# A two-block transformer on one core: the low-part splits of the second block's weights all on VectorE

## The chip, the cores and the metric

The kernel runs on one core of one Trainium2 chip. The time is device microseconds of one execution; a kernel's time is the median of several. One further execution was taken with the profiler, and every row below is from it. Engines are called PE (TensorE matmul), PEld (its weight loads), DVE (VectorE), ACT (ScalarE), POOL (GpSimd) and SP (SyncE), as in the profile.

## The reference

Everything is float32, with 512 tokens of width 1024. A first block (a gated delta-rule branch and a windowed-attention branch over 512 tokens and a context of 256, merged) hands its result `h` to a second block, which has two layers. A layer is

```
h = h + 0.5*rmsnorm(swiglu(rmsnorm(h,g0)), g1)      # feed-forward, 1024 -> 2816 -> 1024
h = h + rmsnorm(mixer(rmsnorm(h,g2)), g3)           # latent attention and dilated attention
h = h + 0.5*rmsnorm(swiglu(rmsnorm(h,g4)), g5)      # a second feed-forward
h = h + rmsnorm((p @ w_ple) * sigmoid(rmsnorm(h,g6) @ w_gate), g7)
```

## The kernel before

Activations lie transposed, features on partitions and tokens along the row. A float32 product is made of three matmuls in float32r: each operand is written as a high part H and a low part L = value - H, and H·H, H·L and L·H are summed in PSUM (`fm`, `acc` at line 87).

**Weights.** Every weight tile of 128x1024 goes the same way, in `w` (lines 70 to 85): a DMA from SP's queue brings it into `wraw`; ACT copies it to `wH` (line 78); then `wL = wraw - wH` is made at line 80, on VectorE where the letter `l` is "v", the default, and on GpSimd where it is "g". In the second block there are 8 pairs of `wH` and `wL` to go round and 3 `wraw`.

**Stages of a layer.** `ffn` runs over the 22 blocks of 128 of the hidden width in three parts (8, 7 and 7), and after each part multiplies by the down weights and adds into `f`. The last down product is made by halves of 256 tokens, so that the norms of the first half run while PE still works on the second. `norms` and `prenorm` are, for a half: a sum of squares over 8 tiles (ACT squares at lines 156 and 159, DVE adds them at line 160, PE sums at line 133), an inverse square root in some 14 tiny DVE instructions (`rsq`, lines 112 to 124), a broadcast by PE (line 141), then for each of 8 tiles DVE's `nt` (line 191) and `h` (line 193) with a new sum of squares; a second inverse square root; and for each of 8 tiles `ny` (line 171), ACT's `xnH` (line 101) and DVE's `xnL` (line 105). Only then has PE an input for the next stage. The next stage begins by halves too: `ffn` takes its first four hidden blocks (8 weight tiles) for the first half and then for the second, `ple` its 8 gate tiles, `mixer` the latent projections and the values of the dilated branch.

**Who splits where.** The letter "g" stands, in the second block, at just these beginnings: 8 tiles at the start of each of the four `ffn` (the calls of `gw` in part 0), 4 tiles `wvd` in each of the two `mixer`, 8 tiles `wpg` in each of the two `ple`: 56 tiles. All other weights of the second block are split on DVE. The first block has 36 tiles on GpSimd.

**Order.** The program is written in the order of the stages, and the compiler's planner (a list scheduler with estimated costs) then decides the order of instructions on each engine, with the program's order as priority. A queue runs strictly in the planned order: an instruction that waits holds back all behind it on its engine. In the trace such splits are seen among the instructions of the norms that precede them in the program.

Of the kernel before, what the change touches and what calls it, by code (L numbers as in the profile page):

```python
# [26 lines left out]
class Kern:  # L27
# [1027 lines left out]
    def ffn(self, l, j, g_out, g_next):  # L1055

        nc, I = self.nc, self.I
        X = (self.xnH, self.xnL)
        with ExitStack() as ctx:
            p = self.pool(ctx, "ffn", 1)  # L1060
            f = self.f
            NA = 4
            A = {}

            def gu(W, ff, c):
                if ff not in A:
                    A[ff] = tuple(p.tile([128, T], F32R, name="a" + z, bufs=9) for z in "HL")
                pg, pu = self.ps("g"), self.ps("x")
                n = c[1] - c[0]
                self.acc(pg[:, :n], self.fm(W[0], X, range(8), 0, c))  # L1070
                self.acc(pu[:, :n], self.fm(W[1], X, range(8), 0, c))
                s = p.tile([128, T], F32, name="fs", bufs=2)[:, :n]
                a = p.tile([128, T], F32, name="fa", bufs=2)[:, :n]
                nc.scalar.activation(s, pg[:, :n], AF.Silu)
                nc.vector.tensor_tensor(a, s, pu[:, :n], op=ALU.mult)  # L1075
                self.split(A[ff][0][:, c[0]:c[1]], A[ff][1][:, c[0]:c[1]], a, h="v")

            def gw(ff, l2="vv"):
                return [self.w(I["gu"][l, j, ff, z], 8, 128, l=l2[z]) for z in range(2)]

            ss = [self.SumSq(self) for _ in HALVES]

            def down(W, part, dm, c):
                k0, k1 = PARTS[part]
                n = c[1] - c[0]
                ps = self.ps("x" if dm % 2 else "g")
                prs = []
                for k in range(k0, k1):
                    aH, aL = A[k]
                    prs += [(W[0][:, k - k0], aH[:, c[0]:c[1]]), (W[0][:, k - k0], aL[:, c[0]:c[1]]),  # L1090
                            (W[1][:, k - k0], aH[:, c[0]:c[1]])]
                self.acc(ps[:, :n], prs)
                fk = f[:, dm, c[0]:c[1]]
                if part == 0:
                    nc.scalar.activation(fk, ps[:, :n], AF.Copy)
                else:
                    nc.vector.tensor_tensor(fk, fk, ps[:, :n], op=ALU.add)
                if part == len(PARTS) - 1:
                    ss[0 if c[0] == 0 else 1].add(fk)

            def dw(part, dm):
                k0, k1 = PARTS[part]
                return self.w(I["dn%d" % part][l, j, dm], k1 - k0, 128)

            for part, (k0, k1) in enumerate(PARTS):
                ffs = list(range(k0, k1))
                if part == 0:
                    ws = {ff: gw(ff, "gg") for ff in ffs[:NA]}
                    for c in HALVES:
                        for ff in ffs[:NA]:  # L1110
                            gu(ws[ff], ff, c)
                            self.pull(4)
                        self.pull()
                    ffs = ffs[NA:]
                for ff in ffs:
                    gu(gw(ff), ff, (0, T))
                if part < len(PARTS) - 1:
                    for dm in range(8):
                        down(dw(part, dm), part, dm, (0, T))
                else:  # L1120
                    ws = [dw(part, dm) for dm in range(8)]
                    for z, c in enumerate(HALVES):
                        for dm in range(8):
                            down(ws[dm], part, dm, c)
                            self.pull(2)
                        self.later(self.norms(ss[z], c, f, g_out, 0.5, g_next))
# [81 lines left out]
    def mixer(self, l, G):  # L1208

        nc, I = self.nc, self.I  # L1210
# [5 lines left out]
        with ExitStack() as ctx:  # L1216
# [5 lines left out]
            gg = p.tile([128, 8], F32, name="gg")  # L1222
# [75 lines left out]
            with ExitStack() as c2:  # L1298
# [5 lines left out]
                latH = p2.tile([128, 3, T], F32R, name="latH")  # L1304
                latL = p2.tile([128, 3, T], F32R, name="latL")
                ws = [self.w(I["win"][l, z], 8, 128) for z in range(3)] + [self.w(I["wkr"][l], 8, 64)]
                wv = [[self.w(I["wvd"][l, g, z], 4, 256, l="g") for z in range(2)] for g in range(2)]
                kr = [p2.tile([32, T], F32, name="kr%d" % z) for z in range(2)]
                for c in HALVES:
                    n = c[1] - c[0]  # L1310
# [138 lines left out]
            ws = []  # L1449
# [20 lines left out]
    def ple(self, l, G, g_next):  # L1470

        nc, I = self.nc, self.I
        X = (self.xnH, self.xnL)
        with ExitStack() as ctx:
            p = self.pool(ctx, "ple", 1)
            f = self.f
            last = g_next is None
            ws, pe = [], []
            for c in HALVES:
                ss = self.SumSq(self)  # L1480
                for dm in range(8):
                    if c[0] == 0:
                        ws.append(self.w(I["wpg"][l, dm], 8, 128, l="g"))
                        pe.append(p.tile([128, T], F32, name="pe", bufs=8))
                        nc.sync.dma_start(pe[dm], self.ple_dram[l, dm])
                    ps = self.ps("x" if dm % 2 else "g")[:, :256]
                    self.acc(ps, self.fm(ws[dm], X, range(8), 0, c))
                    t = p.tile([128, 256], F32, name="pt", bufs=2)
                    nc.scalar.activation(t, ps, AF.Tanh, scale=0.5)
                    fk = f[:, dm, c[0]:c[1]]  # L1490
                    nc.vector.scalar_tensor_tensor(fk, t, 1.0, pe[dm][:, c[0]:c[1]], op0=ALU.add, op1=ALU.mult)
                    ss.add(fk, 0.5)
                    self.pull(2)
                self.later(self.norms(ss, c, f, G[7], 0.5, g_next, out=self.O["out"] if last else None))
# [254 lines left out]
```

## Time and profile before

| | |
|---|---|
| median of 3 runs | 3103.57 us (3096.75 to 3115.26) |
| the profiled execution, its own time | 3092.88 us |
| its span from the first to the last instruction | 3090.7 us |
| granted TensorE clock, mean over the span | 0.948 of full speed |
| PE, DVE, ACT, POOL busy | 90%, 56%, 35%, 15% |

The profiled execution lies 10.7 us under the median of the three runs. Its time is 2.2 us more than its span. A granted clock of 1.0 is 2.4 GHz, and the only other level in this trace is 0.5 (1.2 GHz).

### The profile page before, as it was taken

The page shows a single profiled execution, that of the slowest core. Times are in us where ns is not written, and L with a number is a line of the kernel's source. Part 1 is how long each engine was busy: PE and PEld are TensorE (multiplying, and loading weights), DVE is VectorE, ACT ScalarE, POOL GpSimd, SP SyncE. Part 2 cuts the span into 40 slices and gives each one's busy share as a digit, 9 for nine tenths or more (in the row PEclk, how much of TensorE's full clock was granted, in tenths as well). Part 3 has the DMA queues.
Part 4 walks back from the last instruction along what each step waited for, and adds up shares of the span by engine and source line. Part 5 has one row for each costly group of instructions (what it writes and reads, how often), then busy time and mean ns, then how long its engine had stood idle before and what let it go on. Part 6 is the DMA issues. An engine that isn't in the chain of part 4 may idle for free.

```text
span 3090.7 us, 41787 instructions
## 1 busy us (share of the span) xinstructions
PE 2795.3 (90%) x15792; PEld 2357.2 (76%) x15792; DVE 1727.9 (56%) x3701; ACT 1082.1 (35%) x2078; POOL 460.2 (15%) x361
## 2 busy tenths in 40 slices
PE   6999698998999986978999988999987887999987
PEld 2877577678888984768888888888886667888887
DVE  6678927666333474668423378433375567623357
ACT  3444235533222232664322233222232474322223
POOL 3024212322000022412000022000011332000010
PEclk8999899999999997999999998999998898999998
DMA  5325341433323147743323221333234763233321
GB/s 192 102 98 170 103 147 49 136 134 116 96 89 100 54 145 204 187 155 100 116 92 99 89 83 56 118 94 97 86 108 136 217 200 114 88 96 92 97 78 55
DMA packets 138017, 354.51 MB, mean 115 GB/s; under 512 B 36912, under 2 KB 41392, under 8 KB 136792
## 3 DMA queue, kind: packets, MB, share of 16 engines
q1 hardware_dynamic: 125752, 316.18, 33.9%
q10 hardware_dynamic: 9216, 23.07, 2.3%
q0 software_dynamic: 2848, 12.59, 1.2%
q8 instruction: 124, 2.03, 0.3%
q14 instruction: 77, 0.63, 0.1%
HBM read 296.21 MB, written 55.57 MB: 114 GB/s over the span
## 4 chain that ended last, share of the span: by engine, by line
PE 69%; DVE 15%; issue 6%; DMA 4%; ACT 4%; POOL 2%; SPq 0%; DVEq 0%; ACTq 0%; POOLq 0%
PE psg L87 30%; PE psx L87 27%; PE psn L87 3%; DVE ss L160 2%; PE psx L1196 1%; DVE big L529 1%; DVE wL L80 1%; PE psn L141 1%; DMA wraw<-in_wo 1%; DVE h L193 1%; ACT wH L78 1%; DVE rq_y L120 1%; DVE xnL L105 1%; DVE cy L403 1%; PE psn L133 1%
## 5 line engine op out<-in xcount | busy, mean ns | idle before, releaser
L78 ACT ACTIVATE wH<-wraw 128x1024 fp32r<-128x1024 f32 (+2 forms) x445 | 445.0, 1003 | 1149.5 <-PE psg L87 571.7
L80 DVE TENSOR_TENSOR wL<-wraw,wH 128x1024 fp32r<-128x1024 f32 (+3 forms) x353 | 407.9, 1157 | 452.0 <-ACT wH L78 451.2
L87 PE MATMUL psg<-xnH,wH 128*128 128x512 f32 (+3 forms) x1528 | 544.5, 358 | 13.5 <-ACT ss L156 6.8
L87 PE MATMUL psg<-xnL,wH 128*128 128x512 f32 (+3 forms) x1528 | 544.5, 357 | 9.1 <-DVE xnL L105 9.1
L87 PE MATMUL psg<-xnH,wL 128*128 128x512 f32 (+3 forms) x1528 | 546.4, 358 | 6.3 <-POOL wL L80 5.5
L80 POOL TENSOR_TENSOR wL<-wraw,wH 128x1024 fp32r<-128x1024 f32 x92 | 226.6, 2468 | 1896.6 <-ACT wH L78 1068.8
L87 PE MATMUL psx<-xnH,wL 128*128 128x512 f32 (+1 forms) x1120 | 389.0, 348 | 2.8 <-POOL wL L80 1.7
L87 PE MATMUL psx<-xnH,wH 128*128 128x512 f32 (+1 forms) x1120 | 389.9, 348 | 1.7 <-ACT wH L78 1.6
L87 PE MATMUL psx<-xnL,wH 128*128 128x512 f32 (+1 forms) x1120 | 389.7, 348 | 0.0
L87 PEld LDWEIGHTS psg<-xnH,wH 128*128 128x128 f32 (+2 forms) x1528 | 294.5, 193 | 53.6 <-ACT ss L156 7.2
L87 PEld LDWEIGHTS psg<-xnL,wH 128*128 128x128 f32 (+2 forms) x1528 | 295.3, 193 | 49.8 <-DVE xnL L105 12.0
L87 PEld LDWEIGHTS psg<-xnH,wL 128*128 128x128 f32 (+2 forms) x1528 | 295.4, 193 | 46.9 <-POOL wL L80 6.6
L87 PEld LDWEIGHTS psx<-xnH,wL 128*128 128x128 f32 x1120 | 214.9, 192 | 29.9 <-POOL wL L80 1.9
L87 PEld LDWEIGHTS psx<-xnH,wH 128*128 128x128 f32 x1120 | 215.2, 192 | 28.9 <-ACT wH L78 2.3
L87 PEld LDWEIGHTS psx<-xnL,wH 128*128 128x128 f32 x1120 | 215.1, 192 | 25.8
L1075 DVE TENSOR_TENSOR fa<-fs,psx 128x512 f32<-128x512 f32 (+1 forms) x104 | 62.9, 605 | 269.6 <-PE psx L87 268.7
L87 PE MATMUL psg<-aH,wH 128*128 128x512 f32 (+1 forms) x464 | 160.0, 345 | 0.0
L87 PE MATMUL psg<-aL,wH 128*128 128x512 f32 (+1 forms) x464 | 159.3, 343 | 0.0
L87 PE MATMUL psg<-aH,wL 128*128 128x512 f32 (+1 forms) x464 | 159.0, 343 | 0.0
L87 PE MATMUL psx<-aL,wH 128*128 128x512 f32 (+1 forms) x464 | 158.7, 342 | 0.0
L87 PE MATMUL psx<-aH,wL 128*128 128x512 f32 (+1 forms) x464 | 158.2, 341 | 0.0
L87 PE MATMUL psx<-aH,wH 128*128 128x512 f32 (+1 forms) x464 | 158.2, 341 | 0.0
(568 smaller groups left out, 4792.6 us busy)
## 6 DMA issues: line engine op xcount, KB each, us to landing
wraw<-in_gu SPq DMA_DIRECT2D x176, 512.0 KB
wraw<-in_dn SPq DMA_DIRECT2D x64, 448.0 KB
wraw<-in_dn SPq DMA_DIRECT2D x32, 512.0 KB
wraw<-in_wmod SPq DMA_DIRECT2D x24, 512.0 KB
wraw<-in_wrest ACTq DMA_DIRECT2D x24, 512.0 KB
wraw<-in_wo SPq DMA_DIRECT2D x24, 512.0 KB
wraw<-in_win SPq DMA_DIRECT2D x22, 512.0 KB
kh<-KD SPq DMA_DIRECT2D x32, 256.0 KB
```

Source lines behind the costliest of these rows:

```text
L78: nc.scalar.activation(H[:, :n], raw[:, :n], AF.Copy)
L80: e.tensor_tensor(L[:, :n], raw[:, :n], H[:, :n].bitcast(F32), op=ALU.subtract)
L87: self.nc.tensor.matmul(ps, lhsT=l, rhs=r, start=start and i == 0, stop=stop and i == m - 1)
L105: e.tensor_tensor(L, src, H.bitcast(F32), op=ALU.subtract)
L120: nc.vector.scalar_tensor_tensor(z, b, 1.5, y, op0=ALU.add, op1=ALU.mult)
L133: self.nc.tensor.matmul(ps[:, 2 * c:2 * c + 2], lhsT=a[:, 128 * c:128 * c + 128], rhs=self.ones2[:a.shape[0]], start=i == 0, stop=i == len ...
L141: self.nc.tensor.matmul(ps[:, 128 * c:128 * c + 128], lhsT=rs[:, c:c + 1].to_broadcast([128, 128]), rhs=self.ident, start=True, stop=True)
L160: nc.vector.tensor_tensor(self.a[i], self.a[i], q, op=ALU.add)
L193: nc.vector.tensor_tensor(hk, hk, t, op=ALU.add)
L403: nc.vector.scalar_tensor_tensor(y, cb[:, o + j:o + j + n], cw[:, j:j + 1], y, op0=ALU.mult, op1=ALU.add)
L529: nc.vector.tensor_tensor(tm, A[:112, i:i + 1, i + 1:].to_broadcast([112, n, n]), A[:112, i + 1:, i + 1:].rearrange("q j c -> q c j"), op= ...
L1075: nc.vector.tensor_tensor(a, s, pu[:, :n], op=ALU.mult)
```

## The change

The letter "g" is dropped in the second block at all three places, so that the 56 low parts that GpSimd made are made by VectorE. Nothing else is edited: the tiles, their buffers, the DMAs and ACT's copies stay. The first block keeps its 36 splits on GpSimd, and GpSimd keeps its other work (rotary sums, the scaling of attention weights, some DMA issues).

```diff
-            def gw(ff, l2="vv"):
-                return [self.w(I["gu"][l, j, ff, z], 8, 128, l=l2[z]) for z in range(2)]
+            def gw(ff):
+                return [self.w(I["gu"][l, j, ff, z], 8, 128) for z in range(2)]
...
-                    ws = {ff: gw(ff, "gg") for ff in ffs[:NA]}
+                    ws = {ff: gw(ff) for ff in ffs[:NA]}
...
-                wv = [[self.w(I["wvd"][l, g, z], 4, 256, l="g") for z in range(2)] for g in range(2)]
+                wv = [[self.w(I["wvd"][l, g, z], 4, 256) for z in range(2)] for g in range(2)]
...
-                        ws.append(self.w(I["wpg"][l, dm], 8, 128, l="g"))
+                        ws.append(self.w(I["wpg"][l, dm], 8, 128))
```

## Rows read from the trace of the kernel before

**Rows 1.** The page: busy time by engine; the chain that ended last, by engine.
```profile
PE 2795.3 (90%) x15792; PEld 2357.2 (76%) x15792; DVE 1727.9 (56%) x3701; ACT 1082.1 (35%) x2078; POOL 460.2 (15%) x361
...
PE 69%; DVE 15%; issue 6%; DMA 4%; ACT 4%; POOL 2%; SPq 0%; DVEq 0%; ACTq 0%; POOLq 0%
```

**Rows 2.** Groups by shape, second block: busy us, mean ns, idle before, its releasers.
```profile
L80 DVE TENSOR_TENSOR wL<-wraw,wH 128x1024 fp32r<-128x1024 f32 x222 | 272.1, 1226 | 321.5 <-ACT wH L78 320.9
...
L80 POOL TENSOR_TENSOR wL<-wraw,wH 128x1024 fp32r<-128x1024 f32 x56 | 136.4, 2442 | 1741.1 <-ACT wH L78 923.8 <-DVE rq_a L118 704.7 <-DVE ny L171 44.2
```

**Rows 3.** Eight stretches with these splits: length, PE, PEld, DVE, ACT, POOL busy, clock.
```profile
700.00:736.00 36.00, 27.36 (x208) 26.18 (x208) 30.91 (x55) 16.33 (x30) 19.52 (x8) 0.95 0.33 103
...
1792.00:1834.00 42.00, 27.80 (x210) 26.90 (x209) 37.05 (x74) 16.28 (x30) 19.11 (x8) 0.88 0.37 112
...
sum 384.00, PE 295.90 PEld 284.79 DVE 325.86 ACT 165.49 POOL 137.55; mean PE 36.99 PEld 35.60 DVE 40.73 ACT 20.69 POOL 17.19
```

**Rows 4.** POOL in order of time, first feed-forward end of layer 0: start, length.
```profile
1796.45 2.35 POOL L80 TENSOR_TENSOR wL<-wraw,wH 128x1024 fp32r<-128x1024 f32 x1 [352.25 <-DVE rq_a L118]
```

**Rows 5.** DVE in order of time, the same stretch.
```profile
1796.18 0.16 DVE L118 TENSOR_TENSOR rq_a<-rq_v,rq_y 128x2 f32<-128x2 f32 x1
1796.37 0.16 DVE L119 SCALAR_TENSOR_TENSOR rq_b<-rq_a,rq_y 128x2 f32<-128x2 f32 x1
1796.57 2.25 DVE L120 SCALAR_TENSOR_TENSOR rq_y<-rq_b,rq_y 128x2 f32<-128x2 f32 x1
...
1821.19 2.43 DVE L160 TENSOR_TENSOR ss<-ss,ss_q 128x256 f32<-128x256 f32 x1 [0.29 <-ACT ss_q L159]
```

**Rows 6.** DVE groups of the second block, by shape: busy, mean ns.
```profile
L160 DVE TENSOR_TENSOR ss<-ss,ss_q 128x256 f32<-128x256 f32 x248 | 132.3, 540 | 34.5 <-ACT ss_q L159 33.0
L105 DVE TENSOR_TENSOR xnL<-ny,xnH 128x256 fp32r<-128x256 f32 x160 | 82.0, 551 | 9.1 <-ACT xnH L101 8.6
...
L193 DVE TENSOR_TENSOR h<-h,nt 128x256 f32<-128x256 f32 x112 | 61.8, 578 | 0.0
```

**Rows 7.** The same lines from 700 us on: ns shortest/median/longest.
```profile
L160 DVE TENSOR_TENSOR ss<-ss,ss_q x240: 402/419/2654, 702.6 to 3074.5; 128x256 f32<-128x256 f32 x120
...
L105 DVE TENSOR_TENSOR xnL<-ny,xnH x160: 407/417/2657, 699.9 to 3053.3; 128x256 fp32r<-128x256 f32 x160
...
L193 DVE TENSOR_TENSOR h<-h,nt x112: 405/417/2622, 1070.0 to 3040.0; 128x256 f32<-128x256 f32 x112
```

**Rows 8.** The chain that ended last, 1792 to 1834 us: start, us, what.
```profile
1811.66 2.10 DVE ss L160
1813.76 2.48 DVE h L193
...
1833.47 0.62 PE psg L87 x3
```

**Rows 9.** PE's waits, first feed-forward (690 to 800), then 1780 to 1850: us, times, longest.
```profile
PE psg L87 <- POOL wL L80: 4.5, 3, 1.9
PE psx L87 <- POOL wL L80: 1.7, 1, 1.7
...
PE psn L133 <- DVE ss L160: 7.9, 2, 7.7
```

**Rows 10.** DVE's waits for a split's high part: 1385 to 1450, and 2575 to 2645.
```profile
DVE wL L80 <- ACT wH L78: 5.1, 3, 1.8
...
DVE wL L80 <- ACT wH L78: 4.2, 3, 1.9
```

**Rows 11.** DVE splits at the first mixer's start, then one inside an inverse square root.
```profile
1066.85 1.23 DVE L80 TENSOR_TENSOR wL<-wraw,wH 128x1024 fp32r<-128x1024 f32 x1
...
1392.62 1.23 DVE L80 TENSOR_TENSOR wL<-wraw,wH 128x1024 fp32r<-128x1024 f32 x1 [1.51 <-ACT wH L78]
```

**Rows 12.** ACT's waits with the splits' copies, 1785 to 1835.
```profile
ACT wH L78 <- PE psx L87: 5.8, 2, 4.4
ACT wH L78 <- PE psg L87: 4.7, 2, 2.4
```

## The prediction, made before the changed kernel was built or run

> **What bounds the kernel now.** I read the page first. PE is busy for nine tenths of the span and the chain that ended last lies on it for 69%, on DVE for 15% and on POOL for 2% [rows 1]. So only what PE waits for can be won or lost, and it has to be looked for where the 56 splits stand. Order of time on POOL put them into eight stretches, all at the turn of one stage to the next: six with 8 splits (each feed-forward's start, each gate stage's start), two with 4 (the mixers). Together the stretches are 384 us long, PE works 295.9 us of them and DVE 325.9 [rows 3]. Here PE is idle for 88.1 us, and here DVE, not PE, is the fullest engine: 37.05 of 42 us in the fourth stretch. There PE runs out of the old stage's products while the norms, which make the input of the next stage, go step by step through DVE; its longest waits name a DVE sum [rows 9]. The chain confirms it: from 1796 us to the first matmul of the next stage at 1833 us it runs almost without a break over DVE [rows 8].
>
> Then I laid POOL and DVE of one stretch side by side, and this decides the case. POOL starts a split at 1796.45 and takes 2.35 us [rows 4]. DVE's tiny steps took 0.16 us until then; the one that starts at 1796.57 takes 2.25 us, to within 0.1 us of the end of POOL's split [rows 5]. A sum that usually takes 0.42 us takes 2.43 us beside another split. All eight splits of this stretch have such a stretched DVE instruction, and the long pieces of the chain [rows 8] are these. So a split on POOL is not taken off DVE. DVE stands still for most of it, and loses more than the 1.23 us that the same split takes on DVE itself [rows 2].
>
> **The change part by part.**
>
> *The stall that goes.* Lower bound: the three commonest lines of the norms have medians of 419, 417 and 417 ns [rows 7] and means of 540, 551 and 578 [rows 6]; the excess is 248 x 0.121 + 160 x 0.134 + 112 x 0.161 = 30.0 + 21.4 + 18.0 = 69.4 us, 1.24 us a split. Inverse square root steps, stretched too [rows 5], are not in it. Upper bound: the two stretched instructions of rows 5, 2.25 - 0.16 and 2.43 - 0.42, or 2.0 us a split, 112 us. I take 1.7 us, nearer to the upper, since the tiny steps are missing below: 56 x 1.7 = 95.2 us that DVE gets back.
>
> *The splits that come.* 56 x 1.226 us [rows 2] = 68.7 us on DVE. POOL loses 136.4 us of work, which nobody waits for except in the first stretch. On DVE alone that is 95.2 - 68.7 = 26.5 us less. Nothing hides it: the stalls lie on the chain [rows 8], and the splits will lie among the same instructions. The planner puts a split wherever DVE is free by its estimate, as it did with the mixer's own splits in the midst of the norms [rows 11].
>
> *The part of the splits in DVE's idle time.* DVE is idle for 58.1 us of the 384, or 15% [rows 3], in pieces in which it waits for PE or ACT. Bounds: none of the splits' time falls there, or 58.1 us of it. A split of 1.23 us mostly overlaps such a piece in part; I take the share by chance, 15% of 68.7, or 10.3 us gained.
>
> *The wait that comes.* On POOL a split that waited for ACT's copy held up nobody. On DVE it holds all the norm steps queued behind it, so ACT's next squares, PE's sum and the next stage. Bounds for one split: nothing, as at the first mixer's start [rows 11], and 1.55 us, as the six waits of 9.3 us in all of the output weights' splits at two other turns [rows 10]. One of these stood inside an inverse square root and cost 1.51 us there [rows 11]. What ACT itself waits for in the fourth stretch is a buffer that PE must free, 10.5 us in four waits [rows 12]. But ACT's queue is held by these waits already, and its squares with it, so a good part is in the present time. I take 0.25 us a split, near the lower bound since most splits there had no wait: 14 us lost.
>
> *The first stretch.* Here PE waited for POOL's splits outright, 4.5 + 1.7 = 6.2 us [rows 9]. A split of 1.23 in place of 2.44 us halves that: 3 us gained; bounds 0 and 6.2.
>
> *TensorE's clock.* In the fourth stretch the granted clock is 0.88 on average [rows 3]: with levels of 1.0 and 0.5 that is 10 us of 42 at 1.2 GHz, beside gaps of PE. Shorter gaps should give some of it back. Bounds: none, and half of those 10 us in each of eight stretches, 40 us, which would need no gaps at all. I take 3 us.
>
> *What costs nothing.* The DMAs, their queues and ACT's copies are unchanged in number and order of need. POOL's DMA issues lose what stood ahead of them. The 36 splits of the first block, and POOL's other work, stay as they are.
>
> Sum: -26.5 - 10.3 + 14 - 3 - 3 = -28.8 us. The profiled execution took 3092.9 us (its span and 2.2 us around it), so 3064.1 by its own time. It lay 10.7 us under the median of the runs shown; by that median the forecast is 3075 us.
>
> A rule of the Trainium skill speaks against the change: Perfetto Trace Analysis, Optimizing Scalar/DVE Operations, says that work of a saturated DVE may sensibly be offloaded, even to GpSimd. It adds that the two share a read port, so that moving work between them might not help. By the first half alone the 68.7 us would simply be added to DVE, a result that stands below as the fourth rival. The stretched instructions of rows 5 bear out the second half.
>
> **The rivals.**
>
> *Splits wait at the head of DVE's queue, slower.* Place: the six stretches with 8 splits, where ACT's copy waits for a buffer that PE frees. For it speaks that the planner works with estimates and that these waits exist [rows 10, 12]. Against it: today's POOL stalls, which hit DVE at the moment the copy is done, disturb the planned order more. It decides from 0.25 + 28.8 / 56 = 0.76 us of wait a split on; at the 1.55 us of rows 10 for all 56 the loss is 56 x 1.30 - 28.8 = 44 us, or 3148 us.
>
> *The stalls are hidden, no change.* The stretched instructions might lie beside PE's work, with another wait ending last. For it: PE is at work in 77% of the stretches [rows 3]. Against it: the chain [rows 8]. The time would be 3104 us, 15 more or less.
>
> *The splits vanish in DVE's pauses, a larger gain.* If 58.1 us of them fall into idle time, nothing waits and the two small terms hold, the sum is -95.2 + 10.6 - 6 = -90.6 us. That is more than PE's idle 88.1 us, part of which is the norms' own length; I put it at two thirds of it, 60 us, or 3044 us.
>
> *DVE's stall is not POOL's doing, slower.* Then the change gives nothing back and adds 68.7 - 10.3 + 14 - 6 = 66 us: 3170 us. Against it stands the match in time of rows 4 and 5, eight times in a stretch.
>
> **How the numbers follow.** The forecast, a gain of 10 to 50 us, has 0.57; its centre is the predicted time. The larger gain has 0.10, no change 0.15, waits at the head of the queue 0.15, the fourth 0.03. About 0.5%, or 15.5 us, is what a measurement of this kernel can tell from no change. Faster: 0.10, 0.50 of the forecast and 0.02 of no change's lower edge, 0.62. Within: 0.07 of the forecast, 0.12 of no change and 0.01 of a weak wait, 0.20. Slower: 0.14 + 0.03 and the upper edge of no change, 0.18. The range goes from 3040, the larger gain's middle, to 3112, past no change: outside are half of the larger gain, most of the two slower cases and a little of the others, 2 in 10. The likeliest case alone would be 3055 to 3093.
>
> **What would show it.** Right: no DVE instruction of the norms longer than about 0.5 us in the eight stretches, means of lines 160, 105 and 193 near 0.42 us, 278 splits of 1024 columns on DVE from 680 us on at about 1.23 us; the chain from the sum at 1793 us to the next stage's first matmul shorter than its 40 us by some 3 to 7 us; PE's idle time in the stretches down from 88 to about 60 us; the other stages as they were. Wrong: DVE's waits for the high part in these stretches adding up to more than 40 us (the first rival), PE's gaps as long as before with DVE emptier (the second), or DVE instructions still stretched with no GpSimd work beside them (the fourth). The prediction also fails if the planner, given other costs, sets the norms of the two halves in another order, so that PE gets its first input later.

## The result, and the profile after

The changed kernel takes 3058.61 us (median of 4 runs, 3055.07 to 3066.91) beside 3101.34 us for the kernel before: a ratio of 0.9862, with a 95% interval of 0.9828 to 0.9896, or 42.7 us less. It is faster, as forecast; the range of 3040 to 3112 us holds it, and the forecast of 3075 us was 16 us too slow. The range is 72 us wide and holds the kernel before as well, so that it was hit says little; the sign had a chance of 0.62.

The page of the changed kernel, with the busy time by engine and the chain that ended last by engine:

```profile
span 3054.4 us, 41703 instructions
PE 2800.5 (92%) x15792; PEld 2361.5 (77%) x15792; DVE 1682.6 (55%) x3757; ACT 1083.3 (35%) x2078; POOL 324.0 (11%) x305
...
PE 74%; DVE 12%; issue 4%; DMA 4%; ACT 4%; POOL 2%; SPq 0%; DVEq 0%; ACTq 0%; POOLq 0%
```

DVE ran 56 instructions more and is busy 45.3 us less than in [rows 1]; its share of the chain fell from 15% to 12%. Groups of the second block by shape, with the mean in ns behind the time that they took in sum, show where from:

```profile
L80 DVE TENSOR_TENSOR wL<-wraw,wH 128x1024 fp32r<-128x1024 f32 x279 | 341.3, 1225 | 339.3 <-ACT wH L78 338.9
L160 DVE TENSOR_TENSOR ss<-ss,ss_q 128x256 f32<-128x256 f32 x250 | 103.9, 424 | 31.7 <-ACT ss_q L159 30.4
...
L105 DVE TENSOR_TENSOR xnL<-ny,xnH 128x256 fp32r<-128x256 f32 x160 | 60.5, 420 | 9.1 <-ACT xnH L101 8.8
...
L193 DVE TENSOR_TENSOR h<-h,nt 128x256 f32<-128x256 f32 x112 | 43.4, 419 | 0.0
```

The means of 540, 551 and 578 ns [rows 6] became 424, 420 and 419, within 5 ns of the medians of [rows 7]. The longest `h`, 2622 ns before, is now 425 (ns shortest/median/longest of the line):

```profile
L193 DVE TENSOR_TENSOR h<-h,nt x112: 416/419/425, 1069.9 to 3002.1; 128x256 f32<-128x256 f32 x112
```

In the fourth stretch the first layer's second feed-forward ends and its gate stage begins ([rows 4] call it the first feed-forward, but the weights loaded in it are the gate's). There the chain of the changed kernel (start, us, what) reads:

```profile
1786.80 0.44 DVE ss L160
...
1790.25 1.22 DVE wL L80
1791.47 0.08 DVE rq_y L120
...
1804.56 1.14 DVE wL L80
...
1805.76 3.56 DMA wraw<-in_wpg
...
1809.40 1.06 ACT wH L78
1810.46 0.31 ACT xnH L101
1810.77 0.04 issue
1810.82 0.58 PE psg L87
```

In the kernel before the chain passed the same sum here, and the next stage's first matmul at 1833.47 us [rows 8]:

```profile
1793.02 0.44 DVE ss L160
```

From the sum to that matmul it now takes 24.0 us, before 40.4 us. Splits stand between the steps of an inverse square root, but a step costs 0.2 us again. At its end the chain now runs over a load: behind the split at 1804.56 us it waits 3.56 us for a gate tile, and then for ACT's copy of it. The stretch as a whole, with length, the busy times of PE, PEld, DVE, ACT and POOL, and the granted clock:

```profile
1783.00:1811.00 28.00, 25.38 (x209) 24.66 (x208) 23.40 (x74) 12.47 (x26) 0.00 (x0) 1.00 0.20 59
```

PE works 25.4 of 28 us at a granted clock of 1.00, where it worked 27.8 of 42 us at 0.88 [rows 3]. One forecast loss came too. At the first mixer's start DVE now stands still before a split:

```profile
1093.97 0.16 DVE L118 TENSOR_TENSOR rq_a<-rq_v,rq_y 128x2 f32<-128x2 f32 x1
1102.14 1.23 DVE L80 TENSOR_TENSOR wL<-wraw,wH 128x1024 fp32r<-128x1024 f32 x1 [8.02 <-ACT wH L78]
1103.29 0.15 DVE L119 SCALAR_TENSOR_TENSOR rq_b<-rq_a,rq_y 128x2 f32<-128x2 f32 x1
```

For 8.02 us an inverse square root is held in the middle by a weight tile that has not arrived.

Where the time went, stretch by stretch, is worked out by numbering the 15792 matmuls of each profiled execution by their start and taking the difference to the kernel before of the same number's start, at both ends of a stretch (us; minus is gained). Three of the experiments below stand beside it. The last line is the difference of the spans; the rows add up to it within 0.3 us.

| stretch | splits | changed | only feed-forwards | zeros on GpSimd | both engines |
|---|---|---|---|---|---|
| first block | 0 | +5.0 | +5.3 | +12.4 | +6.8 |
| first feed-forward | 8 | -5.2 | -5.2 | -1.5 | -0.6 |
| first mixer | 4 | +0.9 | -5.0 | -1.7 | +3.7 |
| feed-forward behind it | 8 | -7.1 | -5.7 | -11.1 | +8.4 |
| gate stage, next feed-forward | 16 | -17.8 | -8.3 | -31.6 | +9.1 |
| second mixer | 4 | +2.0 | +1.7 | -1.2 | +8.4 |
| feed-forward behind it | 8 | -8.7 | -6.5 | -15.2 | +4.2 |
| last gate stage | 8 | -5.4 | +1.9 | -13.1 | +10.3 |
| whole span | 56 | -36.3 | -21.5 | -63.1 | +50.1 |

The feed-forwards and gate stages gained, the two mixers lost a little. The steady parts between the stretches agree to 0.1 us. Two further profiles of the changed kernel give the feed-forwards and gate stages again within 2 us (-17.0 and -18.9 for the largest), the mixers between +1.2 and +4.5 us, and the first block +4.9 and -2.7 us. The first block's +5.0 us are therefore not the change's (last section).

### The profile page after: what moved, and what is told of

Its sections match the earlier page's. It is cut to its first block, busy times and chain, and to the rows that moved or that the text cites. A ratio compares the mean times of both kernels' runs of the same rounds, so it can differ in the third digit from the quotient of the medians.

```text
span 3054.4 us, 41703 instructions
## 1 busy us (share of the span) xinstructions
PE 2800.5 (92%) x15792; PEld 2361.5 (77%) x15792; DVE 1682.6 (55%) x3757; ACT 1083.3 (35%) x2078; POOL 324.0 (11%) x305
## 4 chain that ended last, share of the span: by engine, by line
PE 74%; DVE 12%; issue 4%; DMA 4%; ACT 4%; POOL 2%; SPq 0%; DVEq 0%; ACTq 0%; POOLq 0%
PE psg L87 33%; PE psx L87 29%; PE psn L87 3%; PE psx L1196 2%; DVE wL L80 1%; DVE big L529 1%; DMA wraw<-in_wvd 1%; PE psn L141 1%; ACT wH L78 1%; DVE cy L403 1%; DMA wraw<-in_wo 1%; PE psg L1040 1%; PE psn L133 1%; DVE ss L160 1%; DVE big L531 1%
## 5 line engine op out<-in xcount | busy, mean ns | idle before, releaser
L80 DVE TENSOR_TENSOR wL<-wraw,wH 128x1024 fp32r<-128x1024 f32 (+3 forms) x409 | 476.0, 1166 | 469.6 <-ACT wH L78 469.0
L87 PE MATMUL psg<-xnH,wH 128*128 128x512 f32 (+3 forms) x1528 | 547.5, 360 | 13.9 <-ACT xnH L101 10.3
L87 PEld LDWEIGHTS psg<-xnH,wL 128*128 128x128 f32 (+2 forms) x1528 | 295.6, 193 | 41.5 <-DVE wL L80 1.4
```

Source lines behind the costliest of these rows:

```text
L80: e.tensor_tensor(L[:, :n], raw[:, :n], H[:, :n].bitcast(F32), op=ALU.subtract)
L87: self.nc.tensor.matmul(ps, lhsT=l, rhs=r, start=start and i == 0, stop=stop and i == m - 1)
```

## The experiments

**The changed kernel again**, as a reference in two sets of runs.

> The changed kernel once more, as the reference for the others on the same chip. Expected 3050 to 3068 us beside 3095 to 3112 for the kernel before, a ratio of 0.983 to 0.990.

> The changed kernel a third time, as the reference for the others on the same chip. Expected 3050 to 3068 us, a ratio of 0.983 to 0.990 to the kernel before.

Measured: 3060.93 us, ratio 0.9884 (0.9860 to 0.9907), and 3062.33 us, ratio 0.9874 (0.9851 to 0.9896). The gain repeats.

**GpSimd only writes.** The kernel before, with zeros in place of the 56 low parts:

```diff
-        e.tensor_tensor(L[:, :n], raw[:, :n], H[:, :n].bitcast(F32), op=ALU.subtract)
+        e.tensor_tensor(...) if l != "m" else [nc.gpsimd.memset(L[:, a:n].bitcast(F32), 0.0) for a in (0, 0, 512)]
...
-                    ws = {ff: gw(ff, "gg") for ff in ffs[:NA]}
+                    ws = {ff: gw(ff, "mm") for ff in ffs[:NA]}
```

and "m" for "g" at `wvd` and `wpg`.

> The kernel before, but in the second block GpSimd fills the 56 low parts with zeros, in two and a half fills of about 0.95 us each (2.4 us, as long as its split), in place of subtracting: the low part of these tiles is left out of the product. GpSimd is as busy as before, but reads no operand; VectorE gets no split. Theory (a GpSimd instruction that reads its operands holds up VectorE): no stretched VectorE instruction, their means near 0.42 us; VectorE 105 to 120 us less busy than before, about 1615 us; 45 to 75 us faster than before, 3030 to 3058 us. Rival (VectorE is held up by any GpSimd work, or the gain came from the shorter split): the stretched instructions stay, 3090 to 3105 us.

Measured: 3020.25 us, ratio 0.9747 (0.9720 to 0.9774): 78 us faster than before, more than the theory's 45 to 75. The page, and then two lines of DVE, ns shortest/median/longest (the first reads two operands from SBUF, the second one):

```profile
PE 2794.5 (92%) x15792; PEld 2352.0 (78%) x15792; DVE 1633.3 (54%) x3701; ACT 1082.7 (36%) x2078; POOL 458.9 (15%) x473
```

```profile
L193 DVE TENSOR_TENSOR h<-h,nt x112: 415/419/426, 1080.9 to 2977.1; 128x256 f32<-128x256 f32 x112
...
L114 DVE TENSOR_SCALAR rq_j<-rq_i x48: 159/169/1014, 708.4 to 3013.1; 128x2 int32<-128x2 int32 x48
```

GpSimd is as busy as before (458.9 beside 460.2 us), and `h` is never stretched, though 40 of its 112 instructions ran beside a fill. So it is not GpSimd's work as such that holds up an instruction of DVE with two SBUF operands, but its reading. DVE is 94.6 us less busy than before with the same instructions, below the 105 to 120 us expected; the integer steps are still stretched. The rival fell. This kernel also frees the low parts from ACT's copy, and TensorE multiplies by zeros there, so not all of its 78 us need be the stall's.

**The stall given back.** The changed kernel, with GpSimd making the 56 low parts once more, in four pieces each, for nobody:

```diff
-        e.tensor_tensor(L[:, :n], raw[:, :n], H[:, :n].bitcast(F32), op=ALU.subtract)
+        e.tensor_tensor(...); [nc.gpsimd.tensor_tensor(Z, raw[:, a:a + 256], H[:, a:a + 256].bitcast(F32), op=ALU.subtract) for a in (range(0, n, 256) if l == "b" else ())]
...
-                    ws = {ff: gw(ff) for ff in ffs[:NA]}
+                    ws = {ff: gw(ff, "b") for ff in ffs[:NA]}
```

`Z` is a tile of 128x256; `wvd` and `wpg` get "b" too.

> The changed kernel, with VectorE making the 56 low parts, and GpSimd making each of them once more in four pieces of 256 columns into a scratch tile that nobody reads. The order on VectorE, TensorE, ScalarE and SyncE is that of the changed kernel. Theory (GpSimd's reads hold up VectorE): the stretched instructions come back on top of the splits; VectorE 60 to 115 us busier than in the changed kernel, 1740 to 1800 us, and the time goes up by 40 to 90 us, to 3100 to 3150 us. Rival (the gain came from the order or from the shorter split, not from contention): 3055 to 3070 us, as the changed kernel.

Measured: 3138.20 us, ratio 1.0136 (1.0098 to 1.0174): 77 us slower than the changed kernel, and slower than the kernel before. The planned order on the other four engines is that of the changed kernel. The page, and then a line of DVE, ns shortest/median/longest:

```profile
PE 2823.8 (90%) x15792; PEld 2381.6 (76%) x15792; DVE 1770.1 (56%) x3757; ACT 1085.8 (35%) x2078; POOL 538.0 (17%) x529
```

```profile
L193 DVE TENSOR_TENSOR h<-h,nt x112: 407/419/965, 1076.4 to 3087.8; 128x256 f32<-128x256 f32 x112
```

DVE is 87.5 us busier than in the changed kernel. A stretched `h` takes 0.97 us at most, since GpSimd's pieces are shorter than its splits were (shortest/median/longest, ns):

```profile
L80 POOL TENSOR_TENSOR wZ<-wraw,wH x224: 723/798/2551, 711.5 to 3077.3; 128x256 f32<-128x256 f32 x112
```

The pieces take 214 us in all, where the 56 splits took 136.4 [rows 2], and they stretch DVE's own splits too, up to 1.80 us; so the 77 us are not the change's 43 us turned round. The pieces read `wraw` and `wH`, and might have cost time by holding these buffers. The waits from 680 us on (us, times, longest) speak against it; in the changed kernel DVE's splits waited 452.3 us for the copy:

```profile
DVE wL L80 <- ACT wH L78: 446.0, 174, 6.0
...
ACT wH L78 <- POOL wZ L80: 3.5, 2, 2.6
```

Work that nobody uses costs 77 us by its reads beside DVE. The gain of the change is therefore not one of order or of the shorter split.

**Only the feed-forwards.** The changed kernel with `l="g"` put back at `wvd` and `wpg`, so 32 splits on DVE.

> Only the 32 tiles of the four feed-forwards are split on VectorE; the 16 of the gate stages and the 8 of the mixers stay on GpSimd. Theory (each split that leaves GpSimd gives VectorE 2.0 us and costs it 1.23): the gain stays where the feed-forwards begin, 5 to 9 us at each of the four, 20 to 30 us together, 3068 to 3080 us; the gate stages and mixers are as before the change, with stretched instructions there only. Rival (the gain comes from a better order in some one place): a gain out of proportion, under 10 or over 40 us.

Measured: 3070.63 us, ratio 0.9895 (0.9864 to 0.9925), 29.7 us below the kernel before. The gain stands in proportion, and for the most part where the tiles were moved (table): 5 to 8 us at each feed-forward, none at the last gate stage. The first mixer's -5.0 us, where no tile was moved, are not explained.

**The mixers' tiles back on GpSimd.** Only `l="g"` at `wvd`:

```diff
-                wv = [[self.w(I["wvd"][l, g, z], 4, 256) for z in range(2)] for g in range(2)]
+                wv = [[self.w(I["wvd"][l, g, z], 4, 256, l="g") for z in range(2)] for g in range(2)]
```

> The changed kernel with the 4 wvd tiles of each mixer split on GpSimd again (8 of 56). Theory: at the two mixers the change lost 2.9 and 2.3 us, since a split that waited 8.0 and 7.0 us for its late weights stood in front of an inverse square root on VectorE. With these on GpSimd those waits go and three stalls of 2 us come back at each mixer: the mixers' starts become as long as before the change, so 3 to 6 us faster than the changed kernel, 3053 to 3056 us beside 3059. Rival (the mixers' loss comes from the fuller VectorE, not from the wait): the same as the changed kernel or up to 3 us slower, with the waits of the copy still there.

Measured: 3049.82 us, ratio 0.9852 (0.9829 to 0.9874) beside 0.9884 in the same set. The sign is the theory's, but the intervals overlap, and in the profiled executions of the two the mixers take the same time within 2 us. The waits for the copy did go from DVE. What ACT and PE wait for at the second mixer's start (us, times, longest) tells why that may bring little:

```profile
ACT wH L78 <- DMA wraw<-in_wvd: 6.3, 3, 5.0
...
PE psg L87 <- ACT ss L156: 4.5, 1, 4.5
```

ACT's copy still waits for the late tile, and ACT's squares behind it. By these rows the late load holds up the norms on whichever engine the split stands.

**The loads before the tables.** The mixer's loads of the mask and the rotary tables moved behind `wv = ...`.

> The changed kernel with the mixer's loads of the mask and of the rotary tables issued behind the loads of the wvd tiles, so that three of the four wvd tiles no longer queue behind them. Theory (at the mixer VectorE waits 8.0 and 7.0 us for the late copy of a wvd tile): the waits fall to 3 us or less, each mixer's start gets 3 to 6 us shorter, and the kernel 5 to 12 us faster than the changed one. Rival (the wait is hidden, since TensorE still has the latent projections to do): the waits fall but the time stays within 3 us of the changed kernel.

Measured: 3061.90 us, ratio 0.9873 (0.9847 to 0.9899), as the changed kernel. DVE's waits at the second mixer's start:

```profile
DVE wL L80 <- ACT wH L78: 7.9, 1, 7.9
```

The edit didn't remove the wait, so it doesn't test the theory. Three of the `wvd` loads passed the tables; the fourth, at the first mixer, is issued here:

```profile
1100.06 0.33 SPq L68 DMA_DIRECT2D wraw<-in_wvd  x1
```

That is 5.3 us after the last of the mixer's other loads, and just as the split that began at 1098.78 us gave back one of the three `wraw`. So the fourth load waited for a buffer, no longer for the tables. An earlier load of all four, or more `wraw`, was not tried.

**The first block too.** The changed kernel with the letter dropped at `mod_cols` and `rest` as well: all 92 splits on DVE.

```diff
-                        W = self.w(I["wrest"][z], 8, 128, l="g", q=nc.scalar)
+                        W = self.w(I["wrest"][z], 8, 128, q=nc.scalar)
```

> The changed kernel with the first block's 36 splits on VectorE as well. In the trace of before most of these stretch a VectorE instruction by 0.3 to 1.1 us, or stand where VectorE is idle, so VectorE would get back less than the 1.23 us that each costs. Theory (the sign follows from stall against cost, split by split): no gain, between 0 and 25 us slower than the changed kernel. Rival (splits on VectorE are better everywhere): 10 to 30 us faster than it.

> The kernel with all 92 splits on VectorE once more. It had 3033.7 us beside 3062.3 for the changed kernel and 3100.3 for the one before. If the first block's chain of 62 long multiplications (line 529) sets the end there, and GpSimd's reads stretched it, the gain stays: 3028 to 3042 us, a ratio of 0.976 to 0.982, and TensorE's wait of 24 us for that chain is gone again. If it was the luck of one set of runs, the ratio goes back to 0.985 or more.

Measured: 3033.69 us, ratio 0.9787 (0.9762 to 0.9813), and again 3039.89 us, ratio 0.9811 (0.9784 to 0.9838): 28.6 and some 20 us below the changed kernel. My theory fell and the rival held. DVE is busier, 1689.0 us beside 1683.7 in the changed kernel's profile of the same set, as the theory wanted, but the time went the other way. The chain of 62 multiplications on line 529 and what PE waited for around its end (345 to 385 us) show where it came from. The first two rows are of the changed kernel (third profile), the last of this one, in which the wait is gone:

```profile
L529 DVE TENSOR_TENSOR big<-big x62: 147/819/3740, 294.6 to 391.7; 112x1 f32<-112x1 f32 x2, 112x4 f32<-112x4 f32 x2, 112x9 f32<-112x9 f32 x2, 112x16 f32<-112x16 f32 x2
```

```profile
PE psx L568 <- DVE big L529: 24.1, 1, 24.1
```

```profile
L529 DVE TENSOR_TENSOR big<-big x62: 152/627/1835, 287.4 to 374.7; 112x1 f32<-112x1 f32 x2, 112x4 f32<-112x4 f32 x2, 112x9 f32<-112x9 f32 x2, 112x16 f32<-112x16 f32 x2
```

The last multiplication of the chain starts 17 us earlier; 7 of these 17 us are gained before the chain begins. The 62 multiplications take 47.2 us in place of 67.2, and eleven of the 36 splits now stand between them. The gain is in the first block: numbered as in the table, it is 14.5 and 21.6 us shorter here than in the kernel before. Two readings had misled me. Each shape of the chain occurs twice, so a median over the two was itself stretched, and the stall looked smaller than it is. And DVE's sum over the block doesn't tell which of its instructions lie on the path.

**All but the mixers' tiles.** The last kernel with `l="g"` at `wvd`.

> All splits on VectorE but the 4 wvd tiles of each mixer, which stay on GpSimd. Theory (the wait at the head of VectorE's queue costs the mixers): 3 to 10 us faster than with these 8 on VectorE too. Rival (the late load holds the next stage up on either engine, through ScalarE's copy): within 5 us of it, either way.

Measured: 3033.00 us, ratio 0.9787 (0.9760 to 0.9815), beside 0.9811 for all 92 in the same set: 6.9 us less, within the theory's 3 to 10. It has the lowest median of the versions that leave nothing out of the reference, but is not told apart from all 92. That the 8 tiles do better on GpSimd has now the same sign twice, each time within overlapping intervals, and stays open.

## Why the prediction was right

*The stall that goes.* The mechanism held, and the two experiments on it agree from both sides: without GpSimd's reads it is gone, with them it is back. The size held too. The three commonest lines took 28.4 + 21.5 + 18.4 = 68.3 us less than in [rows 6], for which the lower bound had 69.4. The steps of the inverse square root and the `aL` of line 105 took another 28.5 us less; one of these lines, before and after:

```profile
L120 DVE SCALAR_TENSOR_TENSOR rq_y<-rq_b,rq_y 128x2 f32<-128x2 f32 x96 | 23.4, 244 | 2.5
...
L120 DVE SCALAR_TENSOR_TENSOR rq_y<-rq_b,rq_y 128x2 f32<-128x2 f32 x96 | 15.1, 158 | 1.9
```

That is 96.8 us of stall, 1.7 us a split, where I had 95.2.

*The splits that come.* This term was mis-sized. Each takes 1.225 us, as read from [rows 2], but it does not keep DVE busy for 1.225 us more. Three rows of DVE in the fourth stretch:

```profile
1790.17 0.16 DVE L119 SCALAR_TENSOR_TENSOR rq_b<-rq_a,rq_y 128x2 f32<-128x2 f32 x1
1790.25 1.22 DVE L80 TENSOR_TENSOR wL<-wraw,wH 128x1024 fp32r<-128x1024 f32 x1
1791.39 0.15 DVE L120 SCALAR_TENSOR_TENSOR rq_y<-rq_b,rq_y 128x2 f32<-128x2 f32 x1
```

The split starts 0.08 us before the step ahead of it has ended, and the next step 0.08 us before the split has. Two such steps that follow each other directly start 0.20 us apart [rows 5], with the split between them 1.22 us apart: it costs them 1.02 us. A group's time in [rows 2] and [rows 6] adds up durations; the page's busy time counts once what overlaps. Added up, DVE's durations fell by 26.9 us in the second block, as forecast with 26.5; its busy time there fell by 42.4 us, 15.5 us more. Of these, 9 lie at the ends of splits, the rest where other instructions now follow each other without a pause.

*DVE's idle time: the part in it, and the wait that comes.* The second block between the same two matmuls, the first after 690 us and the last, before and after (length, then the busy times of PE, PEld, DVE, ACT and POOL, the granted clock):

```profile
690.10:3079.40 2389.30, 2186.41 (x12188) 1886.55 (x12186) 1249.16 (x2700) 799.07 (x1502) 281.60 (x240) 0.95 0.37 111
...
695.20:3043.00 2347.80, 2180.82 (x12187) 1883.46 (x12186) 1206.81 (x2756) 800.45 (x1502) 145.42 (x184) 0.95 0.38 113
```

It is 41.5 us shorter: DVE is busy 42.4 us less and idle 0.9 us more. My four terms for what is not DVE's work, -10.3 + 14 - 3 - 3 = -2.3 us, came to +0.9 together. They can't be told apart, but DVE's waits for the copy before splits of 1024 columns rose from 320.9 [rows 2] to 338.9 us, 18 us in place of 14. They are not spread as I had put it: 8.0 and 7.0 us lie at the two mixers, and not at the six stretches with 8 tiles that the first rival named. There I had read the lower bound, nothing, from DVE alone [rows 11]. What ACT waited for in the kernel before, at the first mixer (us, times, longest), showed that the tiles were late:

```profile
ACT wH L78 <- DMA wraw<-in_wvd: 7.3, 3, 6.3
```

*What lies on the chain.* In the fourth stretch the chain lost 16.4 us where I expected 3 to 7. Eight stalls went, but only four of the eight splits now start before the first matmul, two of them on the chain; the other four come behind it.

*The first stretch.* PE waits there no longer for GpSimd; with the stalls it gained 5.2 us.

*TensorE's clock.* In the fourth stretch it is at 1.00 all the time, but over the second block the mean is 0.95 before and after. What it gave back was not separated.

So the gain was half as large again as forecast because DVE's instructions overlap more than before, for the larger part at the splits, and not because a stall is longer. Of the 16 us by which the forecast was slow, 2.2 are its base: the kernel before has a median of 3101.34 us in the result, and had 3103.57 when the forecast was made.

*The rivals.* Waits at the head of DVE's queue came, but not where they were expected and not near the 0.76 us a split at which they would decide: 18 us over 56 are 0.32. That the stalls are hidden is refuted by both experiments on the stall. That they are not GpSimd's doing is refuted by the same. The larger gain did not come. The rule of the Trainium skill that speaks for offloading (Perfetto Trace Analysis, Optimizing Scalar/DVE Operations) fails here by its own proviso on the shared port: the 56 splits on GpSimd cost DVE 96.8 us of stall, and on DVE they take 68.7.

## What to carry to other kernels

GpSimd's elementwise work on SBUF operands is not free beside a busy VectorE: price it by the VectorE instructions that are stretched beside it, not by whether GpSimd is idle, and leave it there only where VectorE has nothing on the path. To see it, lay both engines of one stretch side by side in order of time; compare an instruction with its like when GpSimd rests, not with a median over few that may all be stretched. Don't set a sum of durations against the page's busy time: the first counts twice what overlaps. An in-order queue pays for a late operand with all that stands behind it (8.0 us at one split here), so tiles whose load comes late gain least by a move onto the engine that carries the chain.

## What was not expected of the hardware

*Which instructions wait.* In the kernel before, `nt` (line 191), which reads one operand from SBUF and one from PSUM, ran beside GpSimd's splits 17 times, 7 times wholly within one, and was never stretched (ns shortest/median/longest):

```profile
L191 DVE SCALAR_TENSOR_TENSOR nt<-f,gains,psn x128: 462/474/482, 1069.2 to 3086.4; 128x256 f32<-128x256 f32 x128
```

But the integer steps of the inverse square root, with a single SBUF operand, were, as `rq_j` in the kernel before:

```profile
L114 DVE TENSOR_SCALAR rq_j<-rq_i x47: 157/163/2374, 710.7 to 3076.3; 128x2 int32<-128x2 int32 x47
```

It took up to 2374 ns beside the splits, and up to 1014 ns beside GpSimd's fills, which read nothing (the row of the experiment above), where an instruction with two SBUF operands went through unharmed. The Trainium skill (SBUF — State Buffer, Who interferes with whom) tells it so: an instruction with two SBUF inputs meets only GpSimd's reads, one in a two-port mode meets any GpSimd instruction, one with at most one SBUF input outside these modes none. These rows agree with all three, if line 114 runs in such a mode, which no row shows.

*The same program, two times for one piece.* The first block's instructions up to 430 us are the same in the changed kernel's profiles. In two of them the stretch from 380 to 430 us reads (matmuls in brackets behind the busy time, then PEld, DVE, ACT, POOL, the granted clock):

```profile
380.00:430.00 50.00, 50.00 (x421) 39.33 (x417) 14.64 (x11) 15.18 (x26) 9.99 (x4) 0.73 0.39 101
```

```profile
380.00:430.00 50.00, 50.00 (x561) 39.54 (x558) 15.54 (x11) 19.52 (x34) 11.68 (x5) 0.93 0.41 106
```

PE had stood for 24 us on line 529's chain, to 360 us; the clock was at 1.2 GHz, and rose to 2.4 GHz at 369 to 370 us in both. In the first execution it fell back to 1.2 GHz from 383 to 411 us, in the second not before 420 us:

```profile
383.50:410.50 27.00, 27.00 (x193) 21.00 (x193) 11.24 (x8) 7.31 (x14) 2.80 (x1) 0.50 0.33 74
```

```profile
383.50:410.50 27.00, 27.00 (x302) 21.26 (x301) 12.15 (x8) 11.61 (x21) 6.73 (x3) 1.00 0.49 121
```

PE is busy for the whole 27 us in both; why the clock fell in one is not shown. That moves everything behind it by 8 to 9 us, a fifth of the effect studied here: the difference of two single profiles can't settle anything of that size, and the +5.0 us of the first block in the table are of this kind.
